# Alternating the array's halves in an attention and two low-rank products, and scaling rows in place of diagonal products

## The chip, the cores and the metric

The kernel runs on one core of one Trainium2 chip. The metric is the device time of one execution in microseconds; the time before is the median of three runs.

## What is computed

One layer of a hybrid causal decoder trunk on 256 tokens of width 2048, in float32. Three sub-layers, each with an rmsnorm before and after and a residual:

```python
h = rmsnorm(x, g[0])
z = h @ w_in                                   # columns for the groups A, B, C
oa = rmsnorm(dilated_attention(q, k, v, bias), attn_out_gain)     # A: 12 heads of 64
ob = rmsnorm(spatial_gating(zb, ...), sgu_out_gain)               # B: 8 groups of 64
oc = rwkv7_time_mix(zc, ...)                                      # C: 12 heads of 64
y = concatenate([oa, ob, oc]) @ w_out
x = x + rmsnorm(y, g[1])
x = x + rmsnorm(memory_cross_attention(rmsnorm(x, g[2]), ...), g[3])
x = x + rmsnorm(conv_ffn(rmsnorm(x, g[4]), ...), g[5])
...
# in rwkv7_time_mix
w_log = -softplus(-(w0 + tanh(w_lo) @ w_up)) - 0.5                # w_lo: 64 columns
a = sigmoid(a0 + a_lo @ a_up)                                     # a_lo: 64 columns
```

The change touches the attention (A), the norms behind A and B, and the two low-rank products with w_up and a_up in C.

## The kernel before

**The weight stream.** The weights are read once, in pieces of 128x1024 numbers. A DMA of SyncE brings a piece (`raw`), ScalarE copies it to `hi` (L220), VectorE makes `lo` = raw - hi (L222), and TensorE takes three products of each k tile: hi with the activation's hi, hi with its lo, and lo with its hi. Where the result is wanted as [columns, tokens], `wstat` has them (L252, L254, L257, 256 columns each); where it is wanted as [tokens, columns], `xstat` does (L277, L279, L283, mostly 512 columns each). `raw` has four buffers, `hi` and `lo` three each.

**The side work.** Everything else of the mixer is written as generators, the lanes, which `Lanes` interleaves with the stream: after each piece `advance` runs the lanes whose time has come. A lane yields an estimate in us of how long its next products have to wait for other engines; its products are then queued behind the part of the stream that is traced meanwhile. `drain` runs lanes until a condition holds. The instruction order on each engine comes out of this and of the scheduler's priorities. TensorE, VectorE and ScalarE each take their instructions in that order.

**The low-rank products (`decays`).** For each i of three, `wa` (one buffer, upper 64 partitions w_up, lower 64 a_up, two DMAs from ScalarE's queue) is multiplied with `zl`. L593 writes two products of 64x256 for w_up into one PSUM tile, then two for a_up into another. A float32 product is two instructions on TensorE, so a group is eight.

**The attention (`attention`).** Three blocks j of four heads. A tile of qT and kT holds two heads, one in partitions 0 to 63 and one in 64 to 127. For each head e: scores into a PSUM tile of `auxp` (L1009: 128 columns, L1011: 256 columns, both over 64 rows), bias added and row maxima taken on VectorE (L1014 to L1018), two exponentials on ScalarE (L1020, L1022), `yield 2.5`; then, for the head before it, three transposes (L1030), a copy to SBUF (L1032), `yield 1.5` and the products with v (L1034, L1036, L1038). So there is one head's scores at a time in the stream. `auxp` and `auxq` have two buffers each, `et` (scores and their transposes) four.

**The norms behind A and B.** The rmsnorm factors of a row stand one on each partition. `diag` (L334) multiplies the identity with them, 128x128 on VectorE, and the transposes of the outputs are taken as products with that diagonal: L1063 for A (12 of them), L1139 for B (8), each of 128x128 with 128 columns. That scales and transposes at once.

Of the kernel before, what the change touches and what calls it, by code (L numbers as in the profile page):

```python
# [16 lines left out]
ALU = mybir.AluOpType  # L17
# [44 lines left out]
class Packed:  # L62
    """An activation's transpose [features, tokens], split into hi + lo float32r parts."""
# [43 lines left out]
class Lanes:  # L107
    """Interleaves side work with the weight stream in the order in which it is traced.

    A lane is a generator that yields how long its next products have to wait for other engines (us), or  # L110
    WAIT where it needs a result of the weight stream that is not traced yet. Its products are queued
    behind the part of the weight stream that is traced before them."""
# [36 lines left out]
    def drain(self, until):  # L149
        """Runs the lanes until the condition holds."""  # L150
        while not until():
            n = 0
            for lane in sorted(self.lanes, key=lambda x: x[1])[:]:
                n += self.step(lane)
                if until():
                    return
            assert n or until(), ("lanes are stuck", [(l[0].gi_frame.f_lineno, l[0].gi_yieldfrom.gi_frame.f_lineno if l[0].gi_yieldfrom else 0) for l in self.lanes])


def hybrid_block(tc, a, out, dbg=None):  # L160
    nc = tc.nc
    dbg = dbg or {}
    with ExitStack() as ctx:
# [37 lines left out]
        # ---------------------------------------------------------------- helpers  # L201
# [23 lines left out]
        def units(src, kts, c0, nco):  # L225
            """Yields (position, hi, lo) for pieces of the rows' k tiles (consecutive runs)."""
# [14 lines left out]
        def wstat(src, c0, nco, X, kts=None):  # L241
            """[columns, tokens] tiles of (X^T src[:, c0:c0+nco])^T."""
# [58 lines left out]
        def first_sums(part):  # L301
            """Of four partial sums of squares over a row: the first three, as needed by row_rstd."""
# [10 lines left out]
        def bcast_row(vec, new, eng=None):  # L313
            """Four [P, 512] tiles that hold a [2048] row on every partition."""
# [7 lines left out]
        def put_hi_lo(hi, lo, ps, scale=None):  # L322
            """hi + lo = ps (times a per-partition scale)."""
# [9 lines left out]
        def diag(r, d):  # L333
            nc.vector.tensor_scalar(d, ident, r, None, op0=ALU.mult)  # L334
            return d

        def transposed(X, src, gcol, new):
            """Packed transpose of src * gain; src[token tile][c] are [P, 512] tiles and gcol(k) the gains of
            feature tile k. The factors of rmsnorm, one a token, come with the products (row_factors)."""
# [16 lines left out]
        def row_factors(src, tmp, pins=(None,) * 4):  # L356
            """rmsnorm's factors of the rows of both token tiles: a column each."""
# [13 lines left out]
        def over_rows(r):  # L371
            """The tokens' factors along the free axis, on every partition."""
# [25 lines left out]
        # ---------------------------------------------------------------- input norm  # L398
# [35 lines left out]
        # ---------------------------------------------------------------- constants, small parameters  # L434
# [39 lines left out]
        # relative-position bias: one row of distances per head, in DRAM for Toeplitz reads  # L474
# [42 lines left out]
        # slots of "col" and "v" that the traced work leaves free: the weight stream is not traced past them  # L517
# [57 lines left out]
        def masked(dst, ps, w):  # L575
            """dst [P, n, P] = ps where the mask holds."""
            n = dst.shape[1]
            nc.vector.copy_predicated(dst, msk[:, w:w + 1, :].to_broadcast([P, n, P]), view(ps, n=n, t=P))

        def decays():  # L580
            sgs, As = [], []
            for i in range(3):
# [7 lines left out]
                for dst, key, p0 in ((sg3, "w0", 0), (view(A, c=4, t=P), "a0", 64)):  # L590
                    ps = auxp()
                    for t in range(2):
                        nc.tensor.matmul(ps[:, t * S:(t + 1) * S], lhsT=wa[p0:p0 + 64, t * P:(t + 1) * P],  # L593
                                         rhs=zl[p0:p0 + 64, :], start=True, stop=True)
                    for t in range(2):
# [91 lines left out]
        def inverse():  # L687
            """BN = (I - N)^-1 (transposed) from N (transposed), of all heads and both chunks."""
# [47 lines left out]
            # step j settles the columns of block j  # L736
# [21 lines left out]
        def values(i):  # L758
            """What of heads 4i .. 4i+3 depends on receptance and value, but not on the state."""
# [32 lines left out]
            # token-major: V less its mean over a head, and the bonus term  # L792
# [110 lines left out]
        def outputs(i, c, py, bt, gu3, hv, lv):  # L903
            """Group norm, bonus and gate of one chunk's outputs."""
# [60 lines left out]
        # ---------------------------------------------------------------- (A) dilated attention  # L965
# [21 lines left out]
        def attention():  # L987
# [7 lines left out]
            for j in range(3):  # L995
# [7 lines left out]
                scs = {}  # L1003
                for e in range(5):
                    if e < 4:
                        pr = slice(64 * (e % 2), 64 * (e % 2) + 64)
                        c0 = (e // 2) * S
                        ps = auxp()
                        nc.tensor.matmul(ps[:, 0:128], lhsT=qT[pr, c0:c0 + P], rhs=kT[pr, c0:c0 + P],  # L1009
                                         start=True, stop=True)  # L1010
                        nc.tensor.matmul(ps[:, 128:384], lhsT=qT[pr, c0 + P:c0 + S], rhs=kT[pr, c0:c0 + S],  # L1011
                                         start=True, stop=True)
                        sc = scs[e] = et()
                        nc.vector.tensor_tensor(sc[:, 0:128], ps[:, 0:128], bt[:, e, 128:256], op=ALU.add)  # L1014
                        nc.vector.tensor_tensor(sc[:, 128:384], ps[:, 128:384], bt[:, e, :], op=ALU.add)
                        nmx = small(2)
                        nc.vector.tensor_reduce(nmx[:, 0:1], sc[:, 0:128], axis=AX.X, op=ALU.max, negate=True)
                        nc.vector.tensor_reduce(nmx[:, 1:2], sc[:, 128:384], axis=AX.X, op=ALU.max,  # L1018
                                                negate=True)
                        nc.scalar.activation(sc[:, 0:128], sc[:, 0:128], AF.Exp, bias=nmx[:, 0:1],  # L1020
                                             accum_out=den[:, e:e + 1])
                        nc.scalar.activation(sc[:, 128:384], sc[:, 128:384], AF.Exp, bias=nmx[:, 1:2],  # L1022
                                             accum_out=den[:, 4 + e:5 + e])
                        yield 2.5
                    if e:
                        h = 4 * j + e - 1
                        sc = scs[e - 1]
# [5 lines left out]
                        yield 1.5  # L1033
                        nc.tensor.matmul(ov[:, 0, e - 1, :], lhsT=pT[:, 0:P], rhs=vhead(0, h),  # L1034
                                         start=True, stop=True)
                        nc.tensor.matmul(ov[:, 1, e - 1, :], lhsT=pT[:, P:2 * P], rhs=vhead(0, h),  # L1036
                                         start=True, stop=False)
                        nc.tensor.matmul(ov[:, 1, e - 1, :], lhsT=pT[:, 2 * P:3 * P], rhs=vhead(1, h),  # L1038
# [16 lines left out]
            dgs = s1()  # L1055
            dg = [diag(ars[:, b:b + 1], dgs[:, b * P:(b + 1) * P]) for b in range(2)]
            yield 2.5
            for j in range(3):
                ps = auxp()
                pv = view(ps, k=2, t=S)  # L1060
                for b in range(2):
                    for k in range(2):
                        nc.tensor.matmul(pv[:, k, b * P:(b + 1) * P],  # L1063
                                         lhsT=oas[j][:, b * 256 + k * P:b * 256 + (k + 1) * P], rhs=dg[b],
                                         start=True, stop=True)
# [10 lines left out]
        def gating():  # L1076
# [44 lines left out]
            dg = []  # L1121
            dgs = s1()
            for t in range(2):
# [6 lines left out]
                dg.append(diag(rs, dgs[:, t * P:(t + 1) * P]))  # L1130
# [3 lines left out]
            for j in range(2):  # L1134
                ps = auxq()
                pv = view(ps, k=2, t=S)
                for t in range(2):
                    for k in range(2):
                        nc.tensor.matmul(pv[:, k, t * P:(t + 1) * P],  # L1139
                                         lhsT=pms[t][:, (2 * j + k) * P:(2 * j + k + 1) * P], rhs=dg[t],  # L1140
                                         start=True, stop=True)
# [9 lines left out]
        def qk(j):  # L1151
# [3 lines left out]
            # queries in reverse order inside each block of 128: the bias rows then start at rising offsets  # L1155
# [288 lines left out]
```

## Time and profile before

| | |
|---|---|
| runs | 1393.01, 1389.06, 1388.46 us |
| median | 1389.06 us |
| span of the profiled execution | 1390.5 us |
| granted TensorE clock, mean | 0.993 |
| TensorE, VectorE, ScalarE, GpSimd busy | 98%, 62%, 50%, 6% |

The page lists the time of the profiled execution by its span, from the first instruction to the last; its device time is not given apart from the three runs. A line of the timeline has the start, the busy time, the engine, the line of the kernel, the operation, the output and inputs, rows and columns of the array, the form, and how many instructions were merged (xN); in brackets the idle time ahead and what ended it. Matmuls are pipelined: their issue is read from one start to the next, not from the duration. A line of the groups ends with the busy time and mean duration of one in ns, and the idle time ahead of the group.

The low-rank products lie at 44 to 62 us, the RWKV scores at 80 to 268, the attention at 303 to 420, and the products with diagonals at 426 to 437.

### The profile page before, as it was taken

What the parts mean: (1) busy time and instruction counts of PE and PEld (TensorE: products, weight loads), DVE (VectorE), ACT (ScalarE), POOL (GpSimd) and SP (SyncE); (2) the same over time, 40 slices, a digit from 0 to 9 for tenths busy, and PEclk for the clock granted to TensorE, in tenths of its full rate; (3) what the DMA queues carried; (4) which work ended last, traced back from release to release, by engine and by line L of the source; (5) the groups of instructions that cost most, each with busy time, mean ns of one, the idle gap of its engine ahead of it and who ended that gap; (6) DMA issues with size and microseconds to landing.
All of it is one profiled execution on the core that took longest, in us unless ns stands there. A gap on an engine that the chain in (4) does not pass through costs nothing.

```text
span 1390.5 us, 23314 instructions
## 1 busy us (share of the span) xinstructions
PE 1356.1 (98%) x9432; PEld 1255.6 (90%) x9432; DVE 866.0 (62%) x1273; ACT 688.9 (50%) x1013; POOL 78.4 (6%) x99
## 2 busy tenths in 40 slices
PE   6999999999999999999999999999999999999997
PEld 6889989989988879879999999999999998888886
DVE  5579954456555766567666666666666664444444
ACT  5755372245445656456555555545455453434442
POOL 3011001120002100000000000000000000000001
PEclk9999999999999999998999999999999999999999
DMA  7545553155446855444555555555665666666663
GB/s 231 146 129 164 148 167 87 52 155 149 138 151 201 283 180 170 156 146 136 183 182 182 182 183 182 183 182 184 184 185 183 185 214 193 192 193 193 195 193 130
DMA packets 189849, 238.97 MB, mean 172 GB/s; under 512 B 7920, under 2 KB 144013, under 8 KB 189741
## 3 DMA queue, kind: packets, MB, share of 16 engines
q1 hardware_dynamic: 185802, 225.76, 53.1%
q0 software_dynamic: 3376, 11.29, 2.6%
q8 instruction: 74, 1.21, 0.4%
q10 hardware_dynamic: 563, 0.43, 0.1%
q14 instruction: 34, 0.28, 0.1%
HBM read 235.33 MB, written 2.12 MB: 171 GB/s over the span
## 4 chain that ended last, share of the span: by engine, by line
issue 57%; PE 36%; DMA 2%; DVE 2%; POOL 2%; ACT 1%; ACTq 0%; SPq 0%; DVEq 0%; POOLq 0%
PE mm L252 5%; PE mm L257 5%; PE mm L254 5%; PE mm L277 4%; PE mm L279 4%; PE mm L283 4%; PE auxq L628 1%; DVE lo L222 1%; DMA row<-in_mem_dram 1%; PE auxp L745 1%; PE auxq L745 1%; DMA wa<-in_rwkv_w_up_dram 0%; ACT hi L220 0%; DMA raw<-in_w_in_dram 0%; PE auxq L867 0%
## 5 line engine op out<-in xcount | busy, mean ns | idle before, releaser
L222 DVE TENSOR_TENSOR lo<-raw,hi 128x1024 fp32r<-128x1024 f32 x422 | 516.5, 1225 | 378.3 <-ACT hi L220 373.5
L220 ACT CAST hi<-raw 128x1024 fp32r<-128x1024 f32 x422 | 441.8, 1048 | 466.2 <-PE mm L254 252.3
L252 PE MATMUL mm<-h,hi 128*128 128x256 f32 x2000 | 508.0, 286 | 1.5 <-ACT h L328 1.5
L254 PE MATMUL mm<-h,hi 128*128 128x256 f32 x2000 | 504.8, 285 | 0.3 <-DVE h L329 0.3
L252 PEld LDWEIGHTS mm<-h,hi 128*128 128x128 f32 x2000 | 385.0, 193 | 4.0 <-ACT h L328 1.7
L254 PEld LDWEIGHTS mm<-h,hi 128*128 128x128 f32 x2000 | 385.3, 193 | 1.6 <-issue 0.7
L257 PE MATMUL mm<-h,lo 128*128 128x256 f32 x2000 | 325.4, 285 | 0.0
L257 PEld LDWEIGHTS mm<-h,lo 128*128 128x128 f32 x2000 | 278.0, 193 | 1.9 <-issue 1.0
L277 PE MATMUL mm<-hi,hid 128*128 128x512 f32 x352 | 137.0, 389 | 0.0
L279 PE MATMUL mm<-hi,hid 128*128 128x512 f32 x352 | 137.0, 389 | 0.0
L283 PE MATMUL mm<-lo,hid 128*128 128x512 f32 x352 | 108.3, 389 | 0.0
L1385 ACT ACTIVATE gv<-z,cw 128x256 f32<-128x256 f32 x88 | 53.0, 602 | 71.7 <-DVE z L1384 71.7
L277 PE MATMUL mm<-hi,h 128*128 128x512 f32 (+1 forms) x208 | 79.6, 388 | 0.7 <-ACT hi L220 0.7
L277 PEld LDWEIGHTS mm<-hi,hid 128*128 128x128 f32 x352 | 66.1, 188 | 13.8
L283 PEld LDWEIGHTS mm<-lo,hid 128*128 128x128 f32 x352 | 66.1, 188 | 13.7
L279 PEld LDWEIGHTS mm<-hi,hid 128*128 128x128 f32 x352 | 66.1, 188 | 13.6
L279 PE MATMUL mm<-hi,h 128*128 128x512 f32 (+1 forms) x208 | 76.9, 375 | 0.0
L1386 DVE SCALAR_TENSOR_TENSOR gv<-z,cw,gv 128x255 f32<-128x255 f32 x88 | 42.3, 481 | 29.5 <-ACT gv L1385 29.5
L283 PE MATMUL mm<-lo,h 128*128 128x512 f32 (+1 forms) x208 | 59.8, 375 | 0.2 <-DVE lo L222 0.2
L277 PEld LDWEIGHTS mm<-hi,h 128*128 128x128 f32 x208 | 39.2, 188 | 9.8 <-issue 2.0
L279 PEld LDWEIGHTS mm<-hi,h 128*128 128x128 f32 x208 | 39.2, 189 | 6.0
L283 PEld LDWEIGHTS mm<-lo,h 128*128 128x128 f32 x208 | 37.3, 188 | 8.1 <-DVE lo L222 1.1
(330 smaller groups left out, 1297.8 us busy)
## 6 DMA issues: line engine op xcount, KB each, us to landing
raw<-in_ffn_w_up_dram SPq DMA_DIRECT2D x176, 512.0 KB, 3.7
raw<-in_w_in_dram SPq DMA_DIRECT2D x94, 512.0 KB, 4.2
raw<-in_ffn_w_down_dram SPq DMA_DIRECT2D x88, 512.0 KB, 4.9
raw<-in_w_out_dram SPq DMA_DIRECT2D x32, 512.0 KB, 3.8
raw<-in_mem_wkv_dram SPq DMA_DIRECT2D x16, 512.0 KB, 4.1
raw<-in_mem_wq_dram SPq DMA_DIRECT2D x8, 512.0 KB, 4.5
raw<-in_mem_wo_dram SPq DMA_DIRECT2D x8, 512.0 KB, 3.7
x<-in_x_dram SPq DMA_DIRECT2D x8, 256.0 KB, 6.6
```

What stands on the lines that cost most here:

```text
L220: nc.scalar.copy(hv, rv)
L222: nc.vector.tensor_tensor(lv, rv, hv.bitcast(F32), op=ALU.subtract)
L252: nc.tensor.matmul(o, lhsT=hv[:, k, cs], rhs=X.h(k0 + k), start=(k0 + k == 0), stop=False)
L254: nc.tensor.matmul(o, lhsT=hv[:, k, cs], rhs=X.l(k0 + k), start=False, stop=False)
L257: L.last = nc.tensor.matmul(o, lhsT=lv[:, k, cs], rhs=X.h(k0 + k), start=False, stop=(k0 + k == nk - 1))
L277: nc.tensor.matmul(o, lhsT=X.h(kk)[:, ts_], rhs=hv[:, k, :], start=(first and k0 + k == 0), stop=False)
L279: nc.tensor.matmul(o, lhsT=X.l(kk)[:, ts_], rhs=hv[:, k, :], start=False, stop=False)
L283: L.last = nc.tensor.matmul(o, lhsT=X.h(kk)[:, ts_], rhs=lv[:, k, :], start=False, stop=(last and k0 + k == nk - 1))
L628: nc.tensor.matmul(ps[e][:, n * P:(n + 1) * P], lhsT=l[pr, t0:t0 + P], rhs=r[pr, t0:t0 + P], start=True, stop=True)
L745: nc.tensor.matmul(pv[:, n, c0:], lhsT=BN[:, g * 4 + n, :], rhs=G[g][:, n, c0:], start=True, stop=True)
L1385: nc.scalar.activation(dst, z, AF.Identity, bias=cw[:, 3, n:n + 1], scale=cw[:, 2, n:n + 1])
L1386: nc.vector.scalar_tensor_tensor(dst[:, 1:], z[:, :S - 1], cw[:, 1, n:n + 1], dst[:, 1:], op0=ALU.mult, op1=ALU.add)
```

## The change

Three edits; the rest of the diff takes away comments, so that line numbers are lower by 3 or 4 before the attention.

```diff
@@ decays
-                for dst, key, p0 in ((sg3, "w0", 0), (view(A, c=4, t=P), "a0", 64)):
-                    ps = auxp()
-                    for t in range(2):
+                both = [auxp(), auxp()]
+                for t in range(2):
+                    for ps, p0 in zip(both, (0, 64)):
                         nc.tensor.matmul(ps[:, t * S:(t + 1) * S], lhsT=wa[p0:p0 + 64, t * P:(t + 1) * P],
                                          rhs=zl[p0:p0 + 64, :], start=True, stop=True)
@@ attention
-                for e in range(5):
-                    if e < 4:
-                        pr = slice(64 * (e % 2), 64 * (e % 2) + 64)
-                        c0 = (e // 2) * S
-                        ps = auxp()
-                        nc.tensor.matmul(ps[:, 0:128], lhsT=qT[pr, c0:c0 + P], rhs=kT[pr, c0:c0 + P],
-                                         start=True, stop=True)
-                        nc.tensor.matmul(ps[:, 128:384], lhsT=qT[pr, c0 + P:c0 + S], rhs=kT[pr, c0:c0 + S],
-                                         start=True, stop=True)
...
-                        yield 2.5
-                    if e:
...
-                        yield 1.5
...
+                for e0 in (0, 2):
+                    c0 = (e0 // 2) * S
+                    pss, scs, pts = [auxp(), auxp()], [], []
+                    for q0, k1 in ((0, P), (P, S)):
+                        for e in range(2):
+                            pr = slice(64 * e, 64 * e + 64)
+                            nc.tensor.matmul(pss[e][:, q0:q0 + k1], lhsT=qT[pr, c0 + q0:c0 + q0 + P],
+                                             rhs=kT[pr, c0:c0 + k1], start=True, stop=True)
+                    nmx = small(4)
+                    for e in range(2):
...
+                    yield 4.5
+                    for sc in scs:
+                        pt = auxp()
+                        for b in range(3):
+                            nc.tensor.transpose(pt[:, b * P:(b + 1) * P], sc[:, b * P:(b + 1) * P], ident)
+                        pT = et()
+                        nc.vector.tensor_copy(pT[:, :384], pt[:, :384])
+                        pts.append(pT)
+                    yield 2.0
+                    for e in range(e0, e0 + 2):
...
-            dgs = s1()
-            dg = [diag(ars[:, b:b + 1], dgs[:, b * P:(b + 1) * P]) for b in range(2)]
+            for oa in oas:
+                for b in range(2):
+                    o = oa[:, b * 256:(b + 1) * 256]
+                    nc.vector.tensor_scalar(o, o, ars[:, b:b + 1], None, op0=ALU.mult)
...
-                        nc.tensor.matmul(pv[:, k, b * P:(b + 1) * P],
-                                         lhsT=oas[j][:, b * 256 + k * P:b * 256 + (k + 1) * P], rhs=dg[b],
-                                         start=True, stop=True)
+                        nc.tensor.transpose(pv[:, k, b * P:(b + 1) * P],
+                                            oas[j][:, b * 256 + k * P:b * 256 + (k + 1) * P], ident)
@@ gating
-                dg.append(diag(rs, dgs[:, t * P:(t + 1) * P]))
+                nc.vector.tensor_scalar(mx_, mx_, rs, None, op0=ALU.mult)
...
-                        nc.tensor.matmul(pv[:, k, t * P:(t + 1) * P],
-                                         lhsT=pms[t][:, (2 * j + k) * P:(2 * j + k + 1) * P], rhs=dg[t],
-                                         start=True, stop=True)
+                        nc.tensor.transpose(pv[:, k, t * P:(t + 1) * P],
+                                            pms[t][:, (2 * j + k) * P:(2 * j + k + 1) * P], ident)
```

The per-head work on VectorE and ScalarE (bias, maxima, exponentials) is the same; it is now written for both heads of a pair behind their scores (L1011 to L1019). The transposes are L1027, the products with v L1034 to L1038, the scales L1058 and L1129, the transposes of the outputs L1065 and L1138, the low-rank products L589.

How this moves the instructions. On TensorE at the start of the attention, before: `auxp_531` and `auxp_539` are the scores of the first two heads, `mm_518` and `mm_519` the stream's sums, `auxq_534` a transposed matrix of the gating.

```order
L283 MATMUL mm_519_3175<-lo_528_3203,h_16_122 128x512 x2
L1009 MATMUL auxp_531_3220<-col_466_2871,col_381_2444 128x128
L1011 MATMUL auxp_531_3220<-col_466_2871,col_381_2444 128x256
L1087 MATMUL auxq_534_3231<-ident_97,nat_525_3191 128x128 x4
L277 MATMUL mm_518_3174<-hi_537_3240,h_19_133 128x512
...
L283 MATMUL mm_519_3175<-lo_538_3241,h_19_133 128x512 x2
L1009 MATMUL auxp_539_3256<-col_466_2871,col_381_2444 128x128
L1011 MATMUL auxp_539_3256<-col_466_2871,col_381_2444 128x256
```

And now, on TensorE at the same place, as far as the first transposes of the pair (18 products of the stream lie between):

```order
L283 MATMUL mm_519_3175<-lo_528_3203,h_16_122 128x512 x2
L1006 MATMUL auxp_531_3220<-col_466_2871,col_381_2444 128x128
L1006 MATMUL auxp_532_3221<-col_466_2871,col_381_2444 128x128
L1006 MATMUL auxp_531_3220<-col_466_2871,col_381_2444 128x256
L1006 MATMUL auxp_532_3221<-col_466_2871,col_381_2444 128x256
L1088 MATMUL auxq_536_3241<-ident_97,nat_525_3191 128x128 x4
L277 MATMUL mm_518_3174<-hi_539_3250,h_19_133 128x512
...
L283 MATMUL mm_518_3174<-lo_544_3272,h_22_144 128x512 x2
L1027 MATMUL auxp_545_3281<-ident_97,et_534_3227 128x128
```

The second head's scores have moved up by 12 products of the stream, beside the first head's; both heads' transposes follow in one place.

On TensorE in the low-rank products, before (`auxp_69`, `auxp_70` the first group, `auxp_77`, `auxp_78` the second; the lower number is w_up's):

```order
L257 MATMUL mm_97_542<-h_16_122,lo_100_546 128x256
L593 MATMUL auxp_69_379<-zl_281,wa_66_373 128x256 x2
L593 MATMUL auxp_70_384<-zl_281,wa_66_373 128x256 x2
...
L252 MATMUL mm_97_542<-h_28_166,hi_111_623 128x256
L593 MATMUL auxp_77_425<-zl_281,wa_74_419 128x256 x2
L254 MATMUL mm_97_542<-h_29_167,hi_111_623 128x256
L252 MATMUL mm_97_542<-h_28_166,hi_111_623 128x256
L254 MATMUL mm_97_542<-h_29_167,hi_111_623 128x256
L257 MATMUL mm_97_542<-h_25_155,lo_112_624 128x256
L593 MATMUL auxp_78_430<-zl_281,wa_74_419 128x256 x2
```

And now, on TensorE at the same place:

```order
L589 MATMUL auxp_69_379<-zl_281,wa_66_373 128x256
L589 MATMUL auxp_70_380<-zl_281,wa_66_373 128x256
L589 MATMUL auxp_69_379<-zl_281,wa_66_373 128x256
L589 MATMUL auxp_70_380<-zl_281,wa_66_373 128x256
...
L254 MATMUL mm_96_541<-h_32_178,hi_115_656 128x256
L589 MATMUL auxp_77_425<-zl_281,wa_74_419 128x256 x2
L589 MATMUL auxp_78_426<-zl_281,wa_74_419 128x256 x2
L252 MATMUL mm_96_541<-h_34_188,hi_115_656 128x256
```

The first group alternates. The second, which was in two places, is in one, five products of the stream later than its second half was, and does not alternate; the third, contiguous before, stays so and does not alternate either.

On VectorE ahead of the transposes of the attention's outputs, before (`s1_733` holds the gating's diagonals, `s1_755` the attention's, `small` the factors on their way through GpSimd):

```order
L1044 TENSOR_TENSOR ca_742_4346<-auxq_686_4102,small_741_4344 128x512
L222 TENSOR_TENSOR lo_769_4439<-raw_767_4436,hi_768_4438 128x1024
L293 TENSOR_SCALAR small_747_4362<-small_745_4359 128x1
L1053 TENSOR_REDUCE small_752_4379<-asq_523_3188 128x2
L334 TENSOR_SCALAR s1_733_4313<-ident_97,small_748_4364 128x128
L293 TENSOR_SCALAR small_753_4381<-small_752_4379 128x2
L334 TENSOR_SCALAR s1_755_4385<-ident_97,small_754_4383 128x128 x2
```

And now, on VectorE at the same place:

```order
L222 TENSOR_TENSOR lo_743_4359<-raw_741_4356,hi_742_4358 128x1024
L1053 TENSOR_REDUCE small_724_4294<-asq_523_3188 128x2
L293 TENSOR_SCALAR small_725_4296<-small_724_4294 128x2
L1058 TENSOR_SCALAR ca_571_3409<-ca_571_3409,small_726_4298 128x256 x2
L1058 TENSOR_SCALAR ca_667_4015<-ca_667_4015,small_726_4298 128x256 x2
L1058 TENSOR_SCALAR ca_718_4270<-ca_718_4270,small_726_4298 128x256 x2
```

Six scales stand where two diagonals stood, and the gating's factor, which lay between, now comes after them.

More of the change, by code (lines that the diff above doesn't have):

```diff
@@ L331, in put_hi_lo @@
             return r
-        def diag(r, d):
-            nc.vector.tensor_scalar(d, ident, r, None, op0=ALU.mult)
-            return d
         def transposed(X, src, gcol, new):
@@ L589, in decays @@
                 nc.gpsimd.memset(sg[:, 0:516:129], 0.0)
-                for dst, key, p0 in ((sg3, "w0", 0), (view(A, c=4, t=P), "a0", 64)):
-                    ps = auxp()
-                    for t in range(2):
+                both = [auxp(), auxp()]
+                for t in range(2):
+                    for ps, p0 in zip(both, (0, 64)):
                         nc.tensor.matmul(ps[:, t * S:(t + 1) * S], lhsT=wa[p0:p0 + 64, t * P:(t + 1) * P],
                                          rhs=zl[p0:p0 + 64, :], start=True, stop=True)
+                for dst, key, p0, ps in ((sg3, "w0", 0, both[0]), (view(A, c=4, t=P), "a0", 64, both[1])):
                     for t in range(2):
@@ L1002, in attention @@
                 bt = b12[:, 4 * j:4 * j + 4, :]
-                scs = {}
-                for e in range(5):
-                    if e < 4:
-                        pr = slice(64 * (e % 2), 64 * (e % 2) + 64)
-                        c0 = (e // 2) * S
-                        ps = auxp()
-                        nc.tensor.matmul(ps[:, 0:128], lhsT=qT[pr, c0:c0 + P], rhs=kT[pr, c0:c0 + P],
-                                         start=True, stop=True)
-                        nc.tensor.matmul(ps[:, 128:384], lhsT=qT[pr, c0 + P:c0 + S], rhs=kT[pr, c0:c0 + S],
-                                         start=True, stop=True)
[L1013 to L1018, printed above, removed]
-                                                negate=True)
[L1020 to L1023, printed above, removed]
-                        yield 2.5
-                    if e:
-                        h = 4 * j + e - 1
-                        sc = scs[e - 1]
@@ new lines, in attention @@
+                for e0 in (0, 2):
[8 more added lines that the diff above has]
+                    for e in range(2):
+                        sc = et()
+                        nc.vector.tensor_tensor(sc[:, 0:128], pss[e][:, 0:128], bt[:, e0 + e, 128:256], op=ALU.add)
+                        nc.vector.tensor_tensor(sc[:, 128:384], pss[e][:, 128:384], bt[:, e0 + e, :], op=ALU.add)
+                        nc.vector.tensor_reduce(nmx[:, 2 * e:2 * e + 1], sc[:, 0:128], axis=AX.X, op=ALU.max,
+                                                negate=True)
+                        nc.vector.tensor_reduce(nmx[:, 2 * e + 1:2 * e + 2], sc[:, 128:384], axis=AX.X,
+                                                op=ALU.max, negate=True)
+                        nc.scalar.activation(sc[:, 0:128], sc[:, 0:128], AF.Exp, bias=nmx[:, 2 * e:2 * e + 1],
+                                             accum_out=den[:, e0 + e:e0 + e + 1])
+                        nc.scalar.activation(sc[:, 128:384], sc[:, 128:384], AF.Exp,
+                                             bias=nmx[:, 2 * e + 1:2 * e + 2],
+                                             accum_out=den[:, 4 + e0 + e:5 + e0 + e])
+                        scs.append(sc)
+                    yield 4.5
+                    for sc in scs:
@@ L1032, in attention @@
                         nc.vector.tensor_copy(pT[:, :384], pt[:, :384])
-                        yield 1.5
-                        nc.tensor.matmul(ov[:, 0, e - 1, :], lhsT=pT[:, 0:P], rhs=vhead(0, h),
+                        pts.append(pT)
+                    yield 2.0
+                    for e in range(e0, e0 + 2):
+                        h, pT = 4 * j + e, pts[e - e0]
+                        nc.tensor.matmul(ov[:, 0, e, :], lhsT=pT[:, 0:P], rhs=vhead(0, h),
                                          start=True, stop=True)
-                        nc.tensor.matmul(ov[:, 1, e - 1, :], lhsT=pT[:, P:2 * P], rhs=vhead(0, h),
+                        nc.tensor.matmul(ov[:, 1, e, :], lhsT=pT[:, P:2 * P], rhs=vhead(0, h),
                                          start=True, stop=False)
-                        nc.tensor.matmul(ov[:, 1, e - 1, :], lhsT=pT[:, 2 * P:3 * P], rhs=vhead(1, h),
+                        nc.tensor.matmul(ov[:, 1, e, :], lhsT=pT[:, 2 * P:3 * P], rhs=vhead(1, h),
                                          start=False, stop=True)
@@ L1120, in gating @@
                 yield WAIT
-            dg = []
-            dgs = s1()
             for t in range(2):
```

## The prediction

> **What bounds the kernel now.** First the head of the page and the list of what TensorE waited for.
>
> ```profile
> span 1390.5 us, 23314 instructions
> PE 1356.1 (98%) x9432; PEld 1255.6 (90%) x9432; DVE 866.0 (62%) x1273; ACT 688.9 (50%) x1013; POOL 78.4 (6%) x99
> ```
> ```profile
> PE auxp L420 <- DMA grow<-in_mem_src_gain_dram: 7.5, 1, 7.5
> PE auxp L593 <- DMA wa<-in_rwkv_a_up_dram: 0.7, 1, 0.7
> PE auxp L593 <- DMA wa<-in_rwkv_w_up_dram: 0.4, 1, 0.4
> PE auxp L1063 <- DVE s L334: 0.4, 1, 0.4
> ```
>
> TensorE is busy for 1356.1 of 1390.5 us, and most of the idle rest is at the start (7.5 us for the first DMA) and between the stages. In the lines that the change touches it waits for only 0.7 + 0.4 + 0.4 = 1.5 us. So the weight stream and the side work share one queue that never stands still: a product less is its issue time less on the clock, and a new wait is that much more. Next the table by stage, for the stretch with the attention (300 to 440 us) and for two short stretches near the low-rank products; the columns are length, busy time and count for PE, PEld, DVE, ACT and POOL, then the granted clock.
>
> ```profile
> 48.80:52.20 3.40, 2.26 (x10) 1.69 (x11) 2.17 (x4) 3.09 (x5) 0.00 (x0) 1.00 0.53 165
> 52.20:55.60 3.40, 3.40 (x14) 2.73 (x13) 1.23 (x1) 3.15 (x5) 0.00 (x0) 0.50 0.50 151
> 300.00:440.00 140.00, 139.62 (x886) 122.19 (x884) 82.41 (x145) 70.75 (x125) 5.98 (x11) 1.00 0.49 144
> ```
>
> In the attention's 140 us TensorE is busy for 139.62, VectorE for 82.41 and ScalarE for 70.75. There is room on the other engines, none on TensorE.
>
> **Scores of the heads.** Here is one head alone in the stream of TensorE (start, busy time, line; L1009 and L1011 are the head's scores, the rest the stream).
>
> ```profile
> 307.22 0.62 PE L283 MATMUL mm<-lo,h 128*128 128x512 f32 x2
> 307.76 0.49 PE L1009 MATMUL auxp<-col,col 64*128 64x128 f32 x2
> 308.09 0.60 PE L1011 MATMUL auxp<-col,col 64*128 64x256 f32 x2
> 308.61 0.50 PE L277 MATMUL mm<-hi,h 128*128 128x512 f32 x1
> 308.95 0.39 PE L279 MATMUL mm<-hi,h 128*128 128x512 f32 x1
> 309.18 0.39 PE L277 MATMUL mm<-hi,h 128*128 128x512 f32 x1
> ```
>
> The stream's products start 0.23 us apart (308.95 to 309.18). From 307.22 to 308.95 pass 1.73 us, in which three of them (L283 twice, L277 once) need 0.69. The head costs the other 1.04 us, for four instructions (a float32 product is two). Twelve heads: 12.5 us.
>
> Whether two halves of the array run side by side can be read from two groups that do so already: the RWKV scores (L628), which alternate the halves, and the low-rank products (L593), which don't.
>
> ```profile
> 80.50 1.16 PE L628 MATMUL auxp<-ca,ca 64*128 64x128 f32 x16
> 81.59 0.50 PE L257 MATMUL mm<-h,lo 128*128 128x256 f32 x2
> ```
> ```profile
> 44.19 1.14 PE L593 MATMUL auxp<-zl,wa 64*128 64x256 f32 x8 [0.30 <-ACT zl L942]
> 45.26 0.39 PE L257 MATMUL mm<-h,lo 128*128 128x256 f32 x1
> ```
> ```profile
> 49.20 1.10 PE L593 MATMUL auxp<-zl,wa 64*128 64x256 f32 x4 [0.45 <-DMA wa<-in_rwkv_w_up_dram]
> 50.23 0.39 PE L254 MATMUL mm<-h,hi 128*128 128x256 f32 x1
> 51.71 1.57 PE L593 MATMUL auxp<-zl,wa 64*128 64x256 f32 x4 [0.74 <-DMA wa<-in_rwkv_a_up_dram]
> ```
>
> At L628, 16 instructions take 81.59 - 80.50 = 1.09 us, 0.068 each, below what one alone can do (0.111, worked out below). At L593, eight instructions on both halves take 45.26 - 44.19 = 1.07 us, and four on one half 50.23 - 49.20 = 1.03. The second half costs 0.04 us. So I price a pair of heads at 1.04 + 0.04 = 1.08 us, six pairs at 6.5, and the term is 12.5 - 6.5 = **6.0 us saved**. It is on the path, since nothing else is late in this stretch.
>
> **Low-rank products.** The first group ran side by side although its program order is two upper, two lower; the order's rows show the third just as contiguous. Alternating them, which the order of the change shows for the first group alone, gains nothing that isn't there. The second group is the open one: its halves were apart because each waited for its own DMA. It now stands in one place some 0.6 us of stream later than the lower half did, still behind both DMAs. The bounds: if both have landed, 0.45 + 0.74 of waiting and one visit of 1.03 go, 2.2 us; if the first DMA is issued later, behind the activations ahead of it, up to 0.5 us is lost. TensorE's arrival and the second DMA's landing (51.71) lie about as before, so I take **0**.
>
> The Trainium skill, TensorE: Matmul & The Clock Gate, Part 3 (packing small matmuls), says that matmuls start and end strictly in program order. By that rule eight instructions in the order four upper, four lower would take near 1.03 + 4 x 0.22 = 1.9 us (an estimate from the rows above), and alternating the first group would save 0.8 us, a sum of 8.6 instead of 7.8. The trace disagrees (eight in 1.07 us in that order), and I go by the trace.
>
> **Diagonals against transposes.** First three transposes in the stream, then eight instructions of the product with a diagonal, and the next product's start.
>
> ```profile
> 311.02 0.62 PE L283 MATMUL mm<-lo,h 128*128 128x512 f32 x2
> 311.48 0.49 PE L1030 MATMUL auxp<-ident,et 128*128 128x128 f32 x3
> 311.72 0.48 PE L277 MATMUL mm<-hi,h 128*128 128x512 f32 x1
> 312.04 0.39 PE L279 MATMUL mm<-hi,h 128*128 128x512 f32 x1
> ```
> ```profile
> 431.38 1.06 PE L1063 MATMUL auxp<-s,ca 128*128 128x128 f32 x8
> 432.27 1.06 PE L1139 MATMUL auxq<-s,et 128*128 128x128 f32 x8
> ```
>
> Three transposes: 312.04 - 311.02 = 1.02, less three of the stream's 0.23, is 0.33 us, 0.110 each. Eight instructions with a diagonal: 0.89 us, 0.111 each, and a float32 product is two of them where a transpose is one. L1063 and L1139 together are 12 + 8 = 20 products, 40 instructions; as transposes they are 20. **2.2 us saved** (20 x 0.111), on the path.
>
> What VectorE gets instead: six scales of 128x256 and two of 128x512 for four of 128x128.
>
> ```profile
> L334 DVE TENSOR_SCALAR s<-ident,small 128x128 f32<-128x128 f32 x4 | 1.1, 286 | 2.1 <-POOL small L298 2.1
> L1104 DVE TENSOR_SCALAR k<-k,small,small 128x512 f32<-128x512 f32 x2 | 1.1, 546 | 1.4 <-POOL small L298 1.4
> ```
>
> Between 0.286 and 0.546 a 128x256 scale is some 0.37 us (an estimate), so this is 3.3 us instead of 1.1 on an engine that has 57 us to spare here. Only two scales stand ahead of the first transposes, where two diagonals stood: 0.2 us later, added to a wait of 0.4. Against that the gating's second diagonal and its power no longer stand ahead of the attention's on VectorE and GpSimd. Bounds: 0.4 us gained (the wait gone) to 0.8 lost (all six scales awaited); I take **0**. The gating's two scales fall into the 5.5 us that the attention's three blocks of transposes and the stream between them fill; without that cover they would cost 1.1.
>
> **Two heads' softmax at once.** The pair's transposes now wait for the second head's exponentials, and both heads queue on VectorE and ScalarE. Groups of these engines in the same 140 us (mean ns stands after the busy time):
>
> ```profile
> L222 DVE TENSOR_TENSOR lo<-raw,hi 128x1024 fp32r<-128x1024 f32 x38 | 46.5, 1222 | 32.5 <-ACT hi L220 32.5
> L1015 DVE TENSOR_TENSOR et<-auxp,ze 128x256 f32<-128x256 f32 x12 | 5.0, 414 | 0.0
> L1018 DVE TENSOR_REDUCE small<-et 128x1 f32<-128x256 f32 x12 | 4.9, 408 | 0.0
> L1014 DVE TENSOR_TENSOR et<-auxp,ze 128x128 f32<-128x128 f32 x12 | 3.5, 289 | 9.5 <-PE auxp L1011 9.4
> L1017 DVE TENSOR_REDUCE small<-et 128x1 f32<-128x128 f32 x12 | 3.3, 275 | 0.0
> ```
> ```profile
> L220 ACT CAST hi<-raw 128x1024 fp32r<-128x1024 f32 x38 | 39.8, 1047 | 43.2 <-PE mm L254 15.4 <-PE mm L279 15.2 <-issue 9.8
> L1022 ACT ACTIVATE et<-et,small 128x256 f32<-128x256 f32 x12 | 6.0, 498 | 0.0
> L1020 ACT ACTIVATE et<-et,small 128x128 f32<-128x128 f32 x12 | 4.8, 400 | 10.3 <-DVE small L1017 10.3
> L1020 ACT ACT_TABLE_LOAD x3 | 3.8, 1283 | 0.1
> ```
>
> A head is 0.29 + 0.41 + 0.28 + 0.41 = 1.39 us on VectorE, two are 2.8, and the last exponential adds 0.5: 3.3 us. A split of the stream ahead of it (1.22) and a cast between the exponentials (1.05) make it 5.5. The cover is the stream between scores and transposes: in the order it is 18 products of 512 columns and four transposes at the first two pairs (18 x 0.23 + 0.45 = 4.6 us) and 24 of 512 columns or their equal at the other four (5.5 us). So between 0 and 0.9 us is exposed at two pairs and none at four: 0 to 1.8 us. Nearer to the first, as VectorE and ScalarE are half idle: I take **0.4 lost**.
>
> **The sum.** 6.0 + 2.2 - 0.4 = 7.8 us saved. The profiled span of 1390.5 becomes 1382.7. That span lies 1.4 us above the median of the three times shown, 1389.06, and inside their spread (1388.46 to 1393.01); from the median the forecast is 1389.06 - 7.8 = **1381.3 us**. A measurement of this kernel can tell about 0.3%, 4.2 us, from no change.
>
> **The rivals.**
>
> *Pairs don't overlap in the attention.* The two heads then run one behind the other in one visit: the visit's 1.04 plus a second head's products, 2 x 0.111 + 2 x 0.22 = 0.66 (an estimate: 256 columns as twice 128). Six visits of 1.70 are 10.2, so 2.3 us is saved instead of 6.0, in all 4.1: 1385.0. For it: each head of a pair has its own wait. Against it: L628 and L593 above. Chance 0.06.
>
> *The softmax is exposed at each pair.* Should each of the six pairs lose 0.8 us (one split and one cast more than fits under the cover), 4.8 is given back instead of 0.4: 7.8 - 4.4 = 3.4 saved, 1385.7. For it: the casts that stand between the exponentials wait for TensorE to free a buffer. Against it: the list of TensorE's waits has no row of L1030 for single heads, and four of the six covers are longer than the chain. Chance 0.12. The Trainium skill, TensorEngine Tiling, section PSUM Bottleneck, warns of just this: row tiling speeds up the products but not the engines that empty PSUM.
>
> *Slower than before.* The same chain with two splits (2.44) and two casts (2.1) of the stream in it is 3.3 + 2.44 + 2.1 = 7.8 us; at three pairs the table load of 1.28 comes on top. Exposed: 2 x 3.2 + 4 x 2.3 + 3 x 1.28 = 19.4 us, against 8.2 saved: 1400.3. The point from which it decides: 1.4 us exposed at each pair gives all back, 2.1 makes the kernel slower by 0.3%. Against it: ScalarE's and VectorE's load in this stretch, 70.75 and 82.41 of 140. Chance 0.03.
>
> *The clock.* The 3.4 us at clock 0.50 that follow the two waits at L593 cost 1.7 us. Whether that stretch comes, goes, or another appears is 1.7 us either way, inside the forecast.
>
> **How the numbers follow.** The forecast has 0.79, at 1381.3. Its own bounds: down by 2.2 (second low-rank group), 0.4, 0.4 and 1.7 to 1376.6; up by 0.5, 0.8, 1.4 and 1.7 to 1385.7. All bounds at once are unlikely, and the first two rivals end at 1385.0 and 1385.7, so 1376.6 to 1385.7 holds 8 in 10 and a little more. Faster by over 0.3% (below 1384.9): the forecast but for its upper edge, and a few parts of the first two rivals, 0.82. Within: 0.15. Slower: 0.03.
>
> **What would show it.** Right: a visit of a pair (the eight instructions of L1006) takes about 1.08 us; L1065 and L1138 have 20 instructions in all, about 0.11 us each; TensorE's waits at L1027 stay under 1 us in total; L589's contiguous groups stay at 1.07 us. Wrong: L1006 visits of 1.7 us; waits of TensorE at L1027 for ScalarE of several us; or a stage after 440 us that has changed its length by more than 1.7 us.

## The result and the profile after

The changed kernel takes 1381.73 us in the median of four runs (1379.76 to 1382.83), the kernel before 1391.02 (1388.46 to 1393.01). The ratio is 0.9937 with a 95% interval of 0.9923 to 0.9950: 7.0 to 10.7 us faster. Beside the experiments the same kernel was timed again: 1380.51 against 1391.28 us, ratio 0.9924 (0.9910 to 0.9938). The profiled execution took 1382.32 us, 1.7 more than its span. One execution of `two_two` below (2210.32 us at a mean granted clock of 0.556) and two of the kernel before (7547.39 and 6412.92 us) were slow, and the ratios leave them out.

Head of the page after:

```profile
span 1380.6 us, 23271 instructions
PE 1346.1 (97%) x9412; PEld 1250.1 (91%) x9412; DVE 867.5 (63%) x1277; ACT 685.1 (50%) x1011; POOL 78.7 (6%) x99
```

TensorE has 20 instructions less (9432 to 9412), the 20 that the products with diagonals had over transposes, and is busy 10.0 us less (1356.1 to 1346.1); the span is 9.9 us shorter. VectorE and ScalarE are where they were. So the gain is time in TensorE's queue. Next what TensorE waited for in the changed lines (columns: total us, times, longest), all rows of the list with such a line:

```profile
PE auxp L589 <- DMA wa<-in_rwkv_w_up_dram: 1.5, 1, 1.5
PE auxp L589 <- ACT zl L939: 0.3, 1, 0.3
```

No wait at the pair's transposes (L1027), none ahead of the transposes of the outputs (L1065), where the kernel before lost 0.4; one DMA wait of 1.5 at the second low-rank group where there were two of 0.4 and 0.7. Now a pair of heads in the stream. A visit is what follows from here on: a run of products over 64 rows, half of the array, that stands between products over all 128.

```profile
353.77 0.64 PE L257 MATMUL mm<-h,lo 128*128 128x256 f32 x4
354.34 0.93 PE L1006 MATMUL auxp<-col,col 64*128 64x128 f32 x8
355.20 0.38 PE L252 MATMUL mm<-h,hi 128*128 128x256 f32 x1
355.42 0.28 PE L254 MATMUL mm<-h,hi 128*128 128x256 f32 x1
```

From 353.77 to 355.42 pass 1.65 us; five products of the stream at 0.12 (their spacing at 256 columns) are 0.60. The pair costs 1.05 us, where one head cost 1.04. And the transposes of the outputs:

```profile
410.73 0.62 PE L283 MATMUL mm<-lo,oc 128*128 128x512 f32 x2
411.19 0.60 PE L1065 MATMUL auxp<-ident,ca 128*128 128x128 f32 x4
411.54 0.48 PE L277 MATMUL mm<-hi,oc 128*128 128x512 f32 x1
411.86 0.39 PE L279 MATMUL mm<-hi,oc 128*128 128x512 f32 x1
```

From 410.73 to 411.86 pass 1.13 us; three products of the stream at 0.23 are 0.69. Four transposes cost 0.44 us, 0.11 each; four products with a diagonal, eight instructions, took 0.89.

**A ledger by position in the stream.** Both kernels run the same 8208 products of the weight stream in the same order. So the start of the n-th of them in the kernel before, less its start in another, says how far the other is ahead at that point, whatever stands between. The two columns on the right are differences of the columns before them. Position 201 lies ahead of the second low-rank group, 241 behind it, 1321 ahead of the attention, 2041 behind the attention's last transposes, 8208 is the last product.

| us ahead of before at | 201 | 241 | 1321 | 2041 | 8208 | 201 to 241 | 1321 to 2041 |
|---|---|---|---|---|---|---|---|
| changed kernel | -0.06 | 2.08 | 0.52 | 9.56 | 9.90 | 2.14 | 9.04 |
| the same again | 0.30 | 0.87 | 0.82 | 9.85 | 11.59 | 0.57 | 9.03 |
| heads_only | 1.18 | 2.65 | 2.64 | 9.41 | 9.67 | 1.47 | 6.77 |
| scales_only | 1.17 | 2.62 | 1.03 | 3.04 | 3.49 | 1.45 | 2.01 |
| lowrank_only | 0.07 | 0.86 | 0.86 | 0.86 | 1.90 | 0.79 | 0.00 |
| same_half | 0.29 | 2.32 | 2.30 | 7.41 | 8.26 | 2.03 | 5.11 |
| two_two_again | 1.22 | 1.89 | 1.89 | 10.88 | 12.58 | 0.67 | 8.99 |
| cover_off | 0.77 | 3.13 | 2.87 | 8.42 | 8.87 | 2.36 | 5.55 |

The column 1321 to 2041 repeats to 0.01 us (9.04, 9.03). The start of a run varies by more than a microsecond (-0.06 to 1.22 at 201), and so does the clock (below); from 1321 to 2041 the ledger separates these from the edit, which the times don't. From 201 to 241 it does not: the kernel before has a stretch at half the clock there, and `heads_only` and `scales_only`, whose low-rank products are those of before, gain 1.47 and 1.45 by having none.

### The profile page after: what moved, and what is told of

Its sections match the earlier page's. It is cut to its first block, busy times and chain, and to the rows that moved or that the text cites. A ratio compares the mean times of both kernels' runs of the same rounds, so it can differ in the third digit from the quotient of the medians.

```text
span 1380.6 us, 23271 instructions
## 1 busy us (share of the span) xinstructions
PE 1346.1 (97%) x9412; PEld 1250.1 (91%) x9412; DVE 867.5 (63%) x1277; ACT 685.1 (50%) x1011; POOL 78.7 (6%) x99
## 4 chain that ended last, share of the span: by engine, by line
issue 57%; PE 37%; DVE 2%; POOL 1%; DMA 1%; ACT 1%; ACTq 0%; DVEq 0%; POOLq 0%
PE mm L252 5%; PE mm L257 5%; PE mm L254 5%; PE mm L277 4%; PE mm L279 4%; PE mm L283 4%; PE auxq L625 1%; DMA wa<-in_rwkv_w_up_dram 1%; PE auxq L742 1%; PE auxp L742 1%; DVE lo L222 1%; DMA raw<-in_w_in_dram 0%; PE auxq L864 0%; PE auxp L921 0%; PE auxp L892 0%
## 5 line engine op out<-in xcount | busy, mean ns | idle before, releaser
L283 PEld LDWEIGHTS mm<-lo,hid 128*128 128x128 f32 x352 | 66.1, 188 | 13.7
```

The source lines that it names most:

```text
L283: L.last = nc.tensor.matmul(o, lhsT=X.h(kk)[:, ts_], rhs=lv[:, k, :], start=False, stop=(last and k0 + k == nk - 1))
```

## The experiments

The theory: a visit costs some 1.05 us whether one half of the array works or both, so pairing saves six visits, and a diagonal costs one instruction of 0.111 us more than a transpose. The rivals: only the number of visits counts; products start strictly in program order, so that alternating is what pays; the longer softmax chain costs something that the forecast missed.

### One edit at a time

`heads_only` is the kernel before with the attention's part of the diff, `scales_only` with the diagonals' part, `lowrank_only` with the part in `decays`; each is that part of the diff above.

> Only the attention's pairing; low-rank products and diagonals as before. Theory (the second half of the array is free): 12.15 us of scores become 6.2, so 5.6 to 6.5 us below the kernel before. Rival (only the number of visits counts, the pair's products still follow one another): 2.3 us below.

Measured: 1385.78 us, ratio 0.9961 (0.9947 to 0.9975), 3.5 to 7.4 us faster; 6.77 us in the attention's stretch. The rival's 2.3 is out. Counted visit by visit in the trace, as above, twelve heads cost 12.5 us before and six pairs 6.2: 6.3 saved. Most of the rest is the wait ahead of the products with diagonals, which in the kernel before stood here:

```profile
425.72 0.63 PE L283 MATMUL mm<-lo,oc 128*128 128x512 f32 x2
426.73 1.13 PE L1063 MATMUL auxp<-s,ca 128*128 128x128 f32 x8 [0.38 <-DVE s L334]
```

Two products of the stream need 0.46 us, but 1.01 pass, so the wait, 0.38 as idle time, holds the first start back by 0.55. It is gone in `heads_only`, since the attention's last block now ends ahead of the gating's factors. 6.3 and 0.55 are 6.85, near the 6.77 of the ledger.

> Only the products with diagonals become scales on VectorE and transposes; attention and low-rank products as before. Theory: 20 instructions of 0.111 us less, 2.2 us below the kernel before, 2.8 if the wait ahead of the first transposes (0.6 us of excess) goes as well. Rival (the scales stand on the path and eat it): between 1 us below and 1 us above.

Measured: 1388.53 us, ratio 0.9994 (0.9986 to 1.0003): between 1.9 us faster and 0.4 slower, not told from no change by the times, which stop short of the theory's 2.2 and overlap the rival's range. The ledger decides: 2.01 us, which is the 2.2 of the 20 instructions less what the wait has grown by. That wait has not gone but risen from 0.4 to 0.7, as its row in the list of TensorE's waits shows:

```profile
PE auxp L1061 <- DVE ca L1054: 0.7, 1, 0.7
```

Six scales (L1054 here) do delay the first transposes when the gating still stands ahead of them. With both edits the delay is hidden: 6.77 + 2.01 = 8.78, and the whole change has 9.04, which leaves 2.27 to the scales there.

> Only the low-rank products alternate; everything else as before. Theory: groups that are contiguous already ran side by side, so nothing but the second group can gain, 0 to 0.6 us below the kernel before, and a clock stretch of 1.7 us either way. Rival (alternating is what pairs the halves): about 0.8 us in each alternating group, and more where the group's two waits become one, 2 us or more below.

Measured: 1389.26 us, ratio 0.9995 (0.9986 to 1.0004), no difference by the times; 0.79 us in the ledger, where the half-clock stretch is the same as before's, and nothing elsewhere that belongs to the edit. Its three groups:

```profile
44.14 1.13 PE L593 MATMUL auxp<-zl,wa 64*128 64x256 f32 x8 [0.31 <-ACT zl L943]
51.27 1.54 PE L593 MATMUL auxp<-zl,wa 64*128 64x256 f32 x8 [1.26 <-DMA wa<-in_rwkv_w_up_dram]
60.28 1.14 PE L593 MATMUL auxp<-zl,wa 64*128 64x256 f32 x8
```

The first group alternates and takes 1.13 us busy; before, without alternating, it took 1.14. The rival's 0.8 us isn't there. What gains is the second group: it is one visit of eight instructions, where before there were two visits of 1.0 us each, and one wait of 1.26 where there were 0.45 and 0.74. So putting two visits in one place paid, and the order in it did not.

### Same visits, same half

Pairs of heads 0 and 2, 1 and 3, in the whole change (the indices of bias, sums and outputs follow and are not shown):

```diff
-                for e0 in (0, 2):
-                    c0 = (e0 // 2) * S
+                for e0 in (0, 1):
+                    pr = slice(64 * e0, 64 * e0 + 64)
...
-                            pr = slice(64 * e, 64 * e + 64)
+                            c0 = e * S
```

> The whole change, but a pair is heads 0 and 2, then 1 and 3: both heads of a pair lie in the same half of the rows, so there are six visits as in the whole change, but nothing can run side by side. Theory: a visit takes about 1.04 + 0.66 = 1.70 us, 3.9 us above the whole change in all, and starts of the eight instructions lie 0.11 and 0.22 us apart. Rival (fewer visits are the gain): as fast as the whole change, visits of 1.05 us.

Measured: 1384.47 us, ratio 0.9953 (0.9939 to 0.9968), against 1380.51 for the whole change on the same chip. In the attention's stretch 5.11 us are left of 9.03: 3.92 lost, 3.9 expected. A visit, at the same place as the one shown above:

```profile
353.29 0.64 PE L257 MATMUL mm<-h,lo 128*128 128x256 f32 x4
353.86 1.57 PE L1006 MATMUL auxp<-col,col 64*128 64x128 f32 x8
355.36 0.39 PE L252 MATMUL mm<-h,hi 128*128 128x256 f32 x1
355.59 0.28 PE L254 MATMUL mm<-h,hi 128*128 128x256 f32 x1
```

2.30 less 0.60 is 1.70 us, the figure expected. All six visits cost 10.1 us. So fewer visits alone are worth 12.5 - 10.1 = 2.4 us, and that the halves work side by side 10.1 - 6.2 = 3.9.

### Alternating or not

`two_two` is the whole change with each pair's scores in the order upper, upper, lower, lower:

```diff
-                    for q0, k1 in ((0, P), (P, S)):
-                        for e in range(2):
+                    for e in range(2):
+                        for q0, k1 in ((0, P), (P, S)):
```

> The whole change, but each pair's scores stand in the order upper, upper, lower, lower, contiguous and not alternating. Theory from the low-rank groups (order inside a contiguous group does not matter): visits of 1.05 us, same time as the whole change within 0.5 us. Rival (products start strictly in program order, so alternating is what pays): the lower head starts only with the upper one's last instruction, visits of about 1.5 us, 2.7 us above the whole change in all.

Measured: 1379.29 us, ratio 0.9918 (0.9901 to 0.9936). The trace that is read here is of the same kernel in another run:

> The kernel two_two once more, for a profile at the full clock. Theory (inside a contiguous group the order does not matter): two starts of the scores 10 to 15 ns apart, one of each half, and visits of 1.05 us as in the whole change. Rival (strict program order): the lower head's four starts behind the upper's four, visits of about 1.5 us.

Measured: 1379.70 us, ratio 0.9922 (0.9909 to 0.9935), the whole change has 0.9924 (0.9910 to 0.9938). A visit:

```profile
352.44 0.64 PE L257 MATMUL mm<-h,lo 128*128 128x256 f32 x4
353.00 0.93 PE L1006 MATMUL auxp<-col,col 64*128 64x128 f32 x8
353.87 0.38 PE L252 MATMUL mm<-h,hi 128*128 128x256 f32 x1
354.09 0.28 PE L254 MATMUL mm<-h,hi 128*128 128x256 f32 x1
```

Again 1.65 less 0.60, 1.05 us. The eight starts in the trace, in ns from the first, of this visit, of the whole change's and of same_half's:

```
two_two_again   0  14  214  227  325  339  544  558
whole change    0   7  214  220  325  332  544  550
same_half       0 213  325  437  548  767  983 1198
```

The lower half's products start 13 to 14 ns behind the upper half's although two of the upper's (four instructions) stand ahead of the lower's first. Two starts on one half are never closer than 111 ns in `same_half`, so the two that are 14 ns apart are one of each half. Strict program order across the halves is refuted, here and in the low-rank groups; nothing here shows the order broken within a half.

### The cover of the softmax

```diff
-                    yield 4.5
+                    yield 0.5
...
-                    yield 2.0
+                    yield 0.5
```

> The whole change with the pair's estimates cut from 4.5 and 2.0 us to 0.5 and 0.5, so that its transposes and products with v are queued with less of the stream between. Theory (the chain of two heads' softmax is some 3.3 to 5.5 us and hides only behind the stream between): TensorE waits for ScalarE or VectorE at the transposes, 1 to 3 us at each of six pairs, 6 to 15 us above the whole change, so no faster than the kernel before. Rival (the other engines are idle enough that the distance does not matter): within 1 us of the whole change.

Measured: 1383.20 us, ratio 0.9953 (0.9939 to 0.9967); on the same chip the kernel before had 1390.22. In the attention's stretch 5.55 us of the 9.03 are left: 3.5 lost. Both expectations miss. TensorE's instructions at one place show why:

```profile
358.84 0.33 PE L1034 MATMUL auxq<-v,et 128*128 128x64 f32 x2
359.00 0.39 PE L1036 MATMUL auxq<-v,et 128*128 128x64 f32 x2
359.23 0.39 PE L1038 MATMUL auxq<-v,et 128*128 128x64 f32 x2
359.54 0.49 PE L1006 MATMUL auxp<-col,col 64*128 64x128 f32 x2
359.96 0.44 PE L1027 MATMUL auxp<-ident,et 128*128 128x128 f32 x2
360.33 0.70 PE L1006 MATMUL auxp<-col,col 64*128 64x256 f32 x2
360.95 0.39 PE L252 MATMUL mm<-h,hi 128*128 128x256 f32 x1
```

The scheduler fills the short distance with what is ready, and so tears pairs apart: one head's first product (L1006), two transposes, the head's second product. Of the six pairs three stay whole; the scores are in ten visits that cost 9.1 us, where six cost 6.2. That is 2.9 of the 3.5. Waiting is not what it costs: over the whole stretch TensorE is busy without a gap (columns as in the tables by stage),

```profile
296.00:432.00 136.00, 136.00 (x872) 118.79 (x871) 85.61 (x151) 66.62 (x122) 9.38 (x15) 1.00 0.52 154
```

and only its weight loads wait at L1027 and L1034, 1.8 us in all (1.0 and 0.5 for ScalarE's exponentials, 0.3 for a copy). The other 0.6 was not separated; a start that is late by less than a product's duration does not show as a gap. VectorE's chain is shorter than it was priced, here the eight operations of a pair, first and last:

```profile
353.61 0.29 DVE L1011 TENSOR_TENSOR et<-auxp,ze 128x128 f32<-128x128 f32 x1 [0.46 <-PE auxp L1006]
...
355.39 0.41 DVE L1015 TENSOR_REDUCE small<-et 128x1 f32<-128x256 f32 x1
```

2.19 us from 353.61 to the end, not the 2.8 that eight mean durations add to, since one begins some 0.08 us before the one ahead ends.

### The wait that is left

`wa_two` gives the low-rank weights two buffers and raises the estimate between their groups from 2.0 to 5.0 us, so that buffers and distance change at once; `wa_late` has the two buffers too, and estimates of 15.0 and 4.0 us. The diff is of `wa_two`:

```diff
-                wa = mk(rp, "wa", 1, (P, 256))
+                wa = mk(rp, "wa", 2, (P, 256))
...
-            return mk(rp, "s1", 8, (P, 256))
+            return mk(rp, "s1", 7, (P, 256))
...
-                yield 2.0
+                yield 5.0
```

> The whole change with two buffers for the low-rank weights (one of the eight s1 buffers is given up for the room), so that the second group's weights are loaded long before. The scheduler then puts the second and third groups some ten products behind the first. Theory: the wait of 1.5 us for that DMA at the second group goes, and up to 1.5 us of the end time, unless a wait for ScalarE's sigmoids takes its place at the same spot. Rival: the wait is hidden elsewhere and nothing changes.

Measured: 1389.30 us, ratio 0.9990 (0.9977 to 1.0003): of the gain of 9.3 and 10.8 us only some 1 us is left. The groups, and TensorE's clock in the windows behind the first (the value behind POOL's column):

```profile
44.64 1.14 PE L589 MATMUL auxp<-zl,wa 64*128 64x256 f32 x8
48.53 2.80 PE L589 MATMUL auxp<-zl,wa 64*128 64x256 f32 x8 [1.84 <-ACT oc L594]
53.48 2.07 PE L589 MATMUL auxp<-zl,wa 64*128 64x256 f32 x4
56.63 2.07 PE L589 MATMUL auxp<-zl,wa 64*128 64x256 f32 x4
```
```profile
45.80:49.20 3.40, 1.56 (x9) 1.30 (x10) 2.33 (x3) 3.38 (x7) 0.00 (x0) 1.00 0.07 16
49.20:62.90 13.70, 13.70 (x48) 10.74 (x47) 7.34 (x11) 6.88 (x12) 1.09 (x2) 0.50 0.36 102
```

The DMA wait is gone, and a wait of 1.84 us for the sigmoids stands in its place, earlier; behind it the clock is at 0.50 for 13.7 us. At half the clock that is 6.9 us of work lost. The traces of the whole change have a second stretch of 3.4 us elsewhere (at 260.9, at 52.8), worth 1.7, which this one has not; so some 5 us come on top of theirs, of the 6.7 to 7.0 that `wa_two` has fallen behind by position 2041 (2.85 against 9.56 and 9.85). The rest was not separated. The twelve times point the same way: the one execution with a mean clock of 0.994 took 1382.44 us, the others, at 0.986 to 0.991, took 1386.50 to 1392.37.

> As wa_two (two buffers for the low-rank weights), but with estimates of 15 and 4 us in place of 2 us between the three groups, which leaves some 24 products of the stream between the first and the second group and some 45 to the third; all three alternate. Theory: the DMA of the second group is early and the sigmoids of the first are nearly done, so that the 1.5 us of waiting at the second group shrink below 0.5 and no half-clock stretch of four windows follows: 1.0 to 1.5 us below the whole change by the stream's position after the low-rank products, which the times can hardly tell. Rival (the wait moves to ScalarE's sigmoids as in wa_two): a wait of over 1 us and a half-clock stretch right behind it.

Measured: 1382.85 us, ratio 0.9951 (0.9938 to 0.9964); the whole change had 0.9924. The longest wait left at L589 is 0.64 us, a little above the 0.5 expected, and no half-clock stretch follows, so that part of the theory holds, but the kernel is no faster. Its work in the RWKV part is queued at other places than in the whole change, so the ledger compares nothing in between; at position 2041 it stands at 9.00 against 9.56 and 9.85, although its trace has one half-clock stretch of 3.4 us less ahead of there. So some 2 us of work are lost in between, and what takes them was not separated. No version tried beats the changed kernel by more than the intervals; `two_two` equals it.

## Why the prediction was right, and where its terms were off

Forecast 1381.3 us, range 1376.6 to 1385.7; measured 1381.73 and, again, 1380.51. That the first is so close is luck in part: the forecast took 7.8 us off 1389.06, while the kernel before, timed beside the changed one, had 1391.02 and the saving was 9.3 us. The start was 2.0 too low and the saving 1.5, and the two cancel. By its steps:

- **Scores, 6.0 saved.** 6.3 by the visits (12.5 to 6.2). The price of a pair, 1.04 + 0.04, was taken from the low-rank groups; measured 1.05. Shown by `heads_only`, and by `same_half`, which keeps the visits and loses 3.9 of it. The rival "pairs don't overlap" had priced such a visit at 1.70, which is what `same_half` has.
- **Diagonals, 2.2 saved.** 2.0 alone, in the ledger of `scales_only`, and 2.3 with the pairing. That the scales cost nothing held only because the attention's pairing moved the gating's factors behind them; alone they lengthen the wait by 0.3.
- **The wait ahead of the transposes, taken at 0.** It went, and with it the 0.55 us by which it held the products back, a little beyond the bound of 0.4 that its idle time gave.
- **Softmax of two heads, 0.4 lost.** 0 lost: no wait at L1027. The first pair's transposes stand in ones and twos between products of the stream, but cost 0.67 us like the others' 0.66 (308.07 to 310.12 less six products of 0.23), and two heads' transposes cost that before. The chain was priced too long (2.8 for 2.2 on VectorE).
- **Low-rank products, 0.** 0.6 to 0.8 saved (0.57, 0.67 and 0.79 in the runs whose clock matches that of before in this place), inside the bounds of -2.2 to 0.5, and for the reason given: the second group only.
- **The clock, 1.7 either way.** The changed kernel's profile has no half-clock stretch at the low-rank products but one of 3.4 us at 260.9, so some 1.5 us was gained at one place and as much lost at the other: 2.14 between 201 and 241, of which 0.6 is the low-rank products', and 0.52 left of 2.08 at 1321. The second run has a stretch at the low-rank products as before's, and one of 6.8 us at 616 where before has one of 10.2 at 626; that is why it ends at 11.59 in the ledger and not at 9.90.
- **The rule on program order**, weighed against the trace: the trace's side was right. The sum of 8.6 by the rule is nearer to the 9.3 measured, but not for its reason: the 0.8 us that it named at the first group isn't in `lowrank_only`.

So the mechanism was right and the sum of 7.8 was low by some 1.9 us: the terms measured in the traces are 6.3 + 2.2 + 0.6 + 0.6 = 9.7, where the ledger has 9.04 and about 0.6. Too low were the wait and the second low-rank group, both taken at 0 (0.6 each), the softmax, taken at 0.4 lost, and the scores (0.3).

## What to carry to other kernels

Where a full queue is the bound, price a side product by what it takes out of the stream's spacing, entry and exit included, and not by its duration: a lone head cost 1.04 us for 0.66 us of products, so there are two things to save, visits and the idle half (here 2.4 and 3.9 us). Two products on different halves of the rows need to stand together in the queue, not to alternate; what kept them apart here was the plan that queued one head at a time. And a distance in the queue has two uses: it hides the chain and it holds the pair together, and here a plan that cut it lost the second, without a wait of TensorE.

## What was not expected of the hardware

- Products on the two halves of the rows start side by side (13 to 14 ns apart) even where four instructions of one half stand ahead of the other's first; the traces show the order kept only within a half.
- The half-clock stretches come in lengths of 3.4 us and its multiples (3.4 at 260.9 in the changed kernel, 10.2 at 616 in it and 6.8 at 616 in its second run, 13.7 in `wa_two`), but for the last one, which runs into the end of the kernel. One followed a stretch with TensorE busy for 2.82 of 3.4 us with small products, where the longest wait was 0.58 us:

```profile
257.50:260.90 3.40, 2.82 (x24) 2.57 (x24) 2.75 (x9) 1.30 (x14) 1.01 (x1) 1.00 0.18 25
260.90:264.30 3.40, 3.40 (x21) 3.18 (x21) 2.26 (x8) 0.26 (x3) 1.17 (x1) 0.50 0.36 129
```

  In the same kernel's second run it was absent there; `scales_only` has it, at 260.3. What decides it was not tried; it moves a single profile by some 1.6 us, nearly as much as the scales are worth.
